# One DMA queue for loads and stores, with longer store runs and shorter load runs, in a FiLM scale-and-shift kernel

## The chip, the cores and the metric

The kernel runs on one core of a Trainium2 chip. The metric is the device time of one execution in microseconds (us), as the median of several executions. The profile's span is shorter than that time by some 1.8 us in the profiled run of the kernel before (84.35 against 82.6). Some executions of this one-core kernel fall in a slower state (from 85.8 us up, over 1.5% above the fastest of the same kernel); they are set aside, and only fast runs are compared.

## The reference

```python
def reference(x, conditioning, gamma_proj, beta_proj):   # x: 32 x 512 x 256, float32
    gamma = conditioning @ gamma_proj                    # 32 x 64 times 64 x 256
    beta = conditioning @ beta_proj
    return (x * (1 + gamma[:, None, :]) + beta[:, None, :]).astype(np.float32)
```

Each of 32 batches has one row of scales and one of shifts. The arithmetic is one multiplication and one addition for each element; the bulk of the work is to bring 16.78 MB in and 16.78 MB out.

## The kernel before

The input is cut into four slabs of 4 MB. In a slab each of 128 partitions holds 32 rows of 256 floats, contiguous in memory, so a slab is 32 KB for each partition. All four slabs have their own place on the chip, so no load waits for a buffer.

```python
LOADS = {0: [8, 24]}                 # rows of each load; a slab not listed: one load of 32 rows
GROUP = 16; ON_DVE = 11
...
for n in LOADS.get(s, [ROWS]):       # all loads on the SyncE queue
    nc.sync.dma_start(out=xs[:, r : r + n, :], in_=x_v[s, :, r : r + n, :])
...                                  # scales and shifts: a short chain of matmuls
for r0 in range(0, ROWS, GROUP):     # two groups of 16 rows in each slab
    v = xs[:, r0 : r0 + ON_DVE, :]               # 11 rows on VectorE
    w = xs[:, r0 + ON_DVE : r0 + GROUP, :]       # 5 rows on GpSimd
    nc.vector.scalar_tensor_tensor(out=v, in0=rows(g_p, nv), scalar=1.0, in1=v,
                                   op0=ALU.add, op1=ALU.mult)
    nc.gpsimd.tensor_tensor(out=w, in0=w, in1=rows(g_s, nw), op=ALU.mult)
    nc.vector.tensor_add(out=v, in0=v, in1=rows(b_p, nv))
    nc.gpsimd.tensor_tensor(out=w, in0=w, in1=rows(b_s, nw), op=ALU.add)
    nc.scalar.dma_start(out=o_v[s, :, r0 : r0 + GROUP, :],       # stores on the ScalarE queue
                        in_=xs[:, r0 : r0 + GROUP, :])
```

A row is 1 KB, so a load of 8, 24 or 32 rows moves runs of 8, 24 or 32 KB for each partition, and a store of 16 rows moves runs of 16 KB. In the packet records such a run is one packet, and each of the 16 DMA engines carries 8 of a transfer's 128.

## Time and profile before

| | before |
|---|---|
| time, median of 3 | 84.59 us (84.4 to 85.89; the last in the slower state) |
| span of the profiled run | 82.6 us |
| packet time of the two queues, share of 16 engines | 48.6% + 48.0% |
| VectorE and GpSimd busy | 60% and 56% |
| last VectorE instruction ends | 66.6 us |
| last store packet ends | 81.4 us |

The table is read from the bottom up. Compute is over 15 us before the last byte is out, and the DMA engines are full throughout. The lines themselves are in the prediction. A second source beside the page is used there: the trace has a start and a duration for each of the 2080 DMA packets. I call a load packet *stretched* by what it took over the undisturbed time of its size, and give the sum of this over all packets divided by 16, which is the stretch for each engine.

### The profile page before, as it was taken

Reading aid. Unit: us, or ns where it says so; the run is one execution under the profiler, and the core shown is the slowest. Engines: PE = TensorE matmul, PEld = TensorE weight load, DVE = VectorE, ACT = ScalarE, POOL = GpSimd, SP = SyncE. Lnnn points to the kernel's source line nnn. Section 1 sums busy time; section 2 is a strip of 40 time slices with the busy share of each in tenths; the row PEclk is TensorE's granted clock in tenths of the full one; section 3 lists DMA queues with packets and bytes.
Section 4 is the critical chain, followed back from the end, with each engine's and each line's share of the span. In section 5 each row is a group of like instructions: output and inputs, shape, how many; then the busy total and the mean of one; then the engine's idle time right before and its main releaser. Section 6 shows DMA issues by size and latency. Waiting matters only on the chain.

```text
span 82.6 us, 156 instructions
## 1 busy us (share of the span) xinstructions
PE 9.1 (11%) x10; PEld 2.8 (3%) x10; DVE 49.9 (60%) x18; ACT 3.9 (5%) x9; POOL 46.2 (56%) x22
## 2 busy tenths in 40 slices
PE   0080000899600000000000000000000000000000
PEld 0100000443000000000000000000000000000000
DVE  2011000059999999999999999999999920000000
ACT  0600000034400000000000000000000000000000
POOL 2000000069999999999999999999995000000000
DMA  3899999969969989998889979899999999999992
GB/s 56 337 508 397 389 397 524 460 302 508 508 270 492 508 381 381 413 476 381 381 381 556 460 302 460 381 468 421 429 452 389 468 421 421 460 389 452 437 421 87
DMA packets 2080, 33.69 MB, mean 408 GB/s; under 512 B 288, under 2 KB 416, under 8 KB 416
## 3 DMA queue, kind: packets, MB, share of 16 engines
q1 hardware_dynamic: 720, 16.78, 48.6%
q10 hardware_dynamic: 1360, 16.92, 48.0%
HBM read 16.92 MB, written 16.78 MB: 408 GB/s over the span
## 4 chain that ended last, share of the span: by engine, by line
DVE 49%; DMA 16%; issue 11%; PE 2%; ACTq 1%; ACT 1%
DVE xs L100 30%; DVE xs L103 19%; DMA gbproj<-in_beta_proj_dram 16%; PE gb_p L79 2%; ACTq L50 1%; ACTq L48 0%; ACT gb_s L82 0%; ACT gb_s L85 0%
## 5 line engine op out<-in xcount | busy, mean ns | idle before, releaser
L102 POOL TENSOR_TENSOR xs<-xs,gb_s 128x1280 f32<-128x1280 f32 x8 | 23.0, 2895 | 16.2 <-ACT gb_s L82 16.2
L100 DVE SCALAR_TENSOR_TENSOR xs<-gb_p,xs 128x2816 f32<-128x2816 f32 x8 | 24.7, 3083 | 10.9 <-ACT gb_s L85 10.9
L103 DVE TENSOR_TENSOR xs<-xs,gb_p 128x2816 f32<-128x2816 f32 x8 | 24.7, 3086 | 0.3
L104 POOL TENSOR_TENSOR xs<-xs,gb_s 128x1280 f32<-128x1280 f32 x8 | 23.0, 2893 | 0.0
L79 PE MATMUL gb_p<-gbproj,cond_T 64*128 64x512 f32 x8 | 7.2, 1074 | 8.9 <-DMA gbproj<-in_beta_proj_dram 8.9
L74 DVE COPY cond_T<-cond_T_p 64x512 f32<-64x512 f32 x1 | 0.7, 683 | 4.3 <-PE cond_T_p L72 4.3
L79 PEld LDWEIGHTS gb_p<-gbproj,cond_T 64*128 64x128 f32 x8 | 2.5, 328 | 13.7 <-issue 13.7
L72 PE MATMUL cond_T_p<-rident,cond_s 32*64 32x512 f32 x2 | 1.9, 1065 | 3.9 <-DMA cond_s<-in_conditioning_dram 3.9
L82 ACT ACTIVATE gb_s<-gb_p 128x256 f32<-128x256 f32 x4 | 1.5, 383 | 16.4 <-PE gb_p L79 16.4
L85 ACT COPY gb_s<-gb_p 128x256 f32<-128x256 f32 x4 | 1.5, 367 | 0.0
L82 ACT ACT_TABLE_LOAD x1 | 1.3, 1283 | 2.4 <-issue 2.4
L67 DVE COPY rident<-ident 32x512 f32<-32x512 f32 x1 | 0.4, 416 | 1.2 <-POOL ident masks.py:199 1.2
L72 PEld LDWEIGHTS cond_T_p<-rident,cond_s 32*64 32x64 f32 x2 | 0.3, 202 | 3.9 <-issue 3.9
masks.py:197 POOL MEMSET ident<- 32x32 f32 x1 | 0.1, 114 | 0.3 <-POOLq L121 0.3
masks.py:199 POOL TENSOR_SCALAR_AFFINE_SELECT ident<-ident 32x32 f32<-32x32 f32 x1 | 0.2, 202 | 0.1
L121 POOL MEMSET const-float32-0.0<- 128x1 f32 x1 | 0.1, 103 | 0.2 <-issue 0.2
L121 POOL MEMSET const-bfloat16-1.0<- 128x1 bf16 x1 | 0.1, 106 | 0.0
L121 POOL MEMSET const-uint8-127<- 128x1 uint8 x1 | 0.1, 106 | 0.0
L121 POOL MEMSET const-float32-1.0<- 128x1 f32 x1 | 0.1, 103 | 0.0
## 6 DMA issues: line engine op xcount, KB each, us to landing
out_dram<-xs ACTq DMA_DIRECT2D x8, 2048.0 KB, 18.2
xs<-in_x_dram SPq DMA_DIRECT2D x3, 4096.0 KB, 32.9
xs<-in_x_dram SPq DMA_DIRECT2D x1, 3072.0 KB, 12.2
xs<-in_x_dram SPq DMA_DIRECT2D x1, 1024.0 KB, 4.6
gbproj<-in_gamma_proj_dram ACTq DMA_DIRECT2D x1, 64.0 KB, 9.1
gbproj<-in_beta_proj_dram ACTq DMA_DIRECT2D x1, 64.0 KB, 12.9
cond_s<-in_conditioning_dram ACTq DMA_DIRECT2D x1, 8.0 KB, 3.0
```

The source lines that it names most:

```text
L50: nc.scalar.dma_start(out=gbproj[:, :dim], in_=gamma_proj)
L67: nc.vector.tensor_copy(out=rident.rearrange("p (b g) -> p b g", g=REP), in_=ident.to_broadcast([batch, batch, REP]),)
L72: nc.tensor.matmul(cond_T_p, lhsT=cond_s, rhs=rident, start=True, stop=True)
L74: nc.vector.tensor_copy(out=cond_T, in_=cond_T_p)
L79: nc.tensor.matmul(p_t, lhsT=cond_T[:, s * P : (s + 1) * P], rhs=gbproj, start=True, stop=True)
L82: nc.scalar.activation(out=s_t[:, :dim], in_=p_t[:, :dim], func=mybir.ActivationFunctionType.Identity, bias=1.0, scale=1.0)
L85: nc.scalar.copy(out=s_t[:, dim:], in_=p_t[:, dim:])
L100: nc.vector.scalar_tensor_tensor(out=v, in0=rows(g_p, nv), scalar=1.0, in1=v, op0=ALU.add, op1=ALU.mult)
L102: nc.gpsimd.tensor_tensor(out=w, in0=w, in1=rows(g_s, nw), op=ALU.mult)
L103: nc.vector.tensor_add(out=v, in0=v, in1=rows(b_p, nv))
L104: nc.gpsimd.tensor_tensor(out=w, in0=w, in1=rows(b_s, nw), op=ALU.add)
L121: nc = _bacc.Bacc("TRN2", target_bir_lowering=False, num_devices=1)
```

## The change

The intent is to let loads and stores no longer compete: with all transfers on one queue, the loads come first and the stores follow. The two middle slabs are loaded in two pieces each, so that compute can start on the first half sooner, and stored whole, in fewer and longer runs.

```diff
-    LOADS = {0: [8, 24]}
+    LOADS = {0: [8, 24], 1: [16, 16], 2: [16, 16]}
+    STORES = {0: (16, 32), 3: (16, 32)}
@@
-            nc.scalar.dma_start(out=o_v[s, :, r0 : r0 + GROUP, :],
-                                in_=xs[:, r0 : r0 + GROUP, :])
+            if (r0 + GROUP) in STORES.get(s, (ROWS,)):
+                e0 = max([0] + [e for e in STORES.get(s, (ROWS,)) if e <= r0])
+                e1 = r0 + GROUP
+                nc.sync.dma_start(out=o_v[s, :, e0:e1, :], in_=xs[:, e0:e1, :])
```

## The prediction

> **What bounds the kernel now.** I read the utilisation part of the page first, then the table of DMA queues, then the stretches of the span, then the DMA view cut to three windows, and only then the chain of work that ended last, because the chain alone misleads here.
>
> ```profile
> span 82.6 us, 156 instructions
> ...
> DVE  2011000059999999999999999999999920000000
> ...
> POOL 2000000069999999999999999999995000000000
> DMA  3899999969969989998889979899999999999992
> ...
> q1 hardware_dynamic: 720, 16.78, 48.6%
> q10 hardware_dynamic: 1360, 16.92, 48.0%
> HBM read 16.92 MB, written 16.78 MB: 408 GB/s over the span
> ```
>
> The two compute engines stop two thirds of the way through and start late; the DMA row is full from the second slice to the last but one. The two queues (q1 carries the loads of SyncE, q10 the constants and the stores of ScalarE) together took 48.6 + 48.0 = 96.6% of sixteen engines' span: 0.966 x 82.6 = 79.8 us of packet time on each DMA engine. What is left, 2.8 us, is at the two ends:
>
> ```profile
> 0.00:2.00 2.00, 0.00 (x0) 0.00 (x0) 0.42 (x1) 0.00 (x0) 0.53 (x6) 1.00 0.29 53
> ...
> 48.00:80.00 32.00, 0.00 (x0) 0.00 (x0) 18.48 (x7) 0.00 (x0) 14.97 (x6) 1.00 1.01 431
> 80.00:81.40 1.40, 0.00 (x0) 0.00 (x0) 0.00 (x0) 0.00 (x0) 0.00 (x0) 1.00 0.63 269
> 81.40:82.60 1.20, 0.00 (x0) 0.00 (x0) 0.00 (x0) 0.00 (x0) 0.00 (x0) 1.00 0.00 0
> ```
>
> The columns are the stretch, its length, the busy time of five engines, the clock, and at the end the DMA share and GB/s. The first packet starts near 1.3 us, the last store packet ends at 81.4 us, and 1.2 us pass before the span ends. So between 1.3 and 81.4, which is 80.1 us, an engine's packets fill 79.8: about 0.3 us of true gaps. The clock outside the span is 84.35 (the profiled run) less 82.6, or 1.75 us.
>
> The chain names VectorE for half the span, but it ends with the last VectorE instruction at 66.6 us (63.49 start plus 3.09); the last store was issued at 66.7 and landed 15.1 us later, since it stood in a queue. The kernel is bound by DMA bytes, with compute ahead of the queue.
>
> **What the Trainium skill says, and whether the trace agrees.** "DMA: Bandwidth & Descriptors", section Specifications, gives a fabric ceiling of 435 GB/s for the sixteen engines; the trace's fully used stretch shows 431, so it agrees. The same page, section Issuing engines are not separate DMA queues, says that transfers from several issuing engines run on the same 16 DMA engines and interleave, and that only issue time is saved. That agrees too: in the window 24 to 48 us the loads hold 72.7% and the stores 25.5%, with no more than 100% between them. Its section Queues, rings and completion order says that an engine goes round robin between queues by packet and takes one queue's descriptors in order; so with everything on one queue I expect all loads first, then stores. The trace before fits the first half (loads and stores share that window), but cannot show the second. "Perfetto Trace Analysis", section DMA Optimizations, suggests giving inputs and outputs different issuing engines when the spread is dynamic, which is what before does and the change undoes; no run here shows yet what that is worth.
>
> **The three regimes in the trace before.** The windows 2 to 24, 24 to 48 and 48 to 80 us are loads alone, loads and stores mixed, and stores alone:
>
> ```profile
> DMA packets 659, 9.47 MB, mean 430 GB/s; under 512 B 128, under 2 KB 256, under 8 KB 256
> ```
> ```profile
> DMA packets 416, 9.96 MB, mean 415 GB/s; under 512 B 32, under 2 KB 32, under 8 KB 32
> ...
> q1 hardware_dynamic: 240, 7.34, 72.7%
> q10 hardware_dynamic: 176, 2.62, 25.5%
> ```
> ```profile
> DMA packets 953, 13.78 MB, mean 431 GB/s; under 512 B 112, under 2 KB 112, under 8 KB 112
> ```
>
> The reader is to see 430, 415 and 431 GB/s. Packets are counted whole where they start, so an edge misplaces up to half a megabyte; the 415 is softer than it looks. The trace's record of single packets is sharper. An undisturbed load packet takes 309 ns for 8 KB, 912 for 24 KB and 1213 for 32 KB; the 1024 store packets of 16 KB take 611. All four lie on one line, 7.7 ns + 37.67 ns per KB (16 KB: 7.7 + 602.7 = 610.4). Load packets of 32 KB longer than 1213 ns cost 0.57 us in sum for each engine: about 0.12 at 12 to 14 us, beside the constants, and 0.45 at 24 to 34 us, around the arrival of the first store (issued 25.9, first packet 29.8).
>
> **The change part by part.**
>
> *Splitting two slabs' loads into 16 KB runs.* Each DMA has 8 packets on each engine. Two 32 KB loads become four of 16 KB: 16 packets become 32 on each engine. By the line above that adds 16 x 7.7 ns = 0.12 us.
>
> *Whole-slab stores for the middle slabs.* Four 16 KB stores become two of 32 KB: 32 packets become 16, which removes 16 x 7.7 ns = 0.12 us. The completion packets (9 ns each) go from 8 to 6 for the stores and from 5 to 7 for the loads. The sum of these parts is zero; the total stays 2080 packets.
>
> *One queue.* The loads no longer share with stores. Their packets: 8 x 0.365 (the 8 KB ones as measured, start-up included) + 8 x 0.937 + 32 x 0.611 + 8 x 1.213 = 2.92 + 7.50 + 19.55 + 9.70 = 39.7 us, plus 0.5 for the constants and 1.3 for the start: all loads are in by about 41.5 us, where before the last ended at 48.6. Then come 32 x 0.611 + 16 x 1.213 = 39.0 us of stores, to 80.5, plus the 0.3 of gaps and 0.1 of completion packets: 80.9, against 81.4. If all the disturbance at 24 to 34 us goes, the gain is 0.45 us; it began before the first store packet ran, so I count on half or a little more, 0.3 to 0.4.
>
> *Readiness.* The order of instructions in the changed build interleaves slabs on VectorE (multiply of the next group ahead of the add of the last). VectorE begins an instruction each 3.065 us from 17.52 (the last of 16 begins at 63.49), so the n-th ends at 17.52 + 3.065(n-1) + 3.09. GpSimd ends its share earlier: it starts at 17.3, 2.85 apart, and its last ends at 63.0. The stores' last operands are GpSimd's third and VectorE's fifth, ninth, 12th, 14th and 16th instruction: ready at 25.9, 32.9, 45.1, 54.3, 60.5 and 66.6. The queue reaches them at 41.5, 46.4, 51.3, 61.0, 70.7 and 75.6 (4.9 us for 2 MB, 9.7 for 4 MB). The slack is 15.6, 13.5, 6.2, 6.7, 10.2 and 9.0 us. The first constant took 3.0 us from issue to landing with little ahead of it, so a start of 2 to 3 us fits inside the smallest. The whole-slab store costs slack, not time. The changed build's waits show no store waiting for another store.
>
> *Start.* The second projection lands at 14.6 us because its packets alternate with 24 and 32 KB load packets; with 16 KB runs it may land up to 1 us sooner. Compute is not on the bounding path, so this only adds slack.
>
> The sum: 84.59 - 0.4 = **84.2 us**.
>
> **The rivals.**
>
> 1. *The queue runs dry.* A store waits in order on SyncE, so the second slab's store, kept back until the whole slab is done, could leave the engines idle and delay all after it. For it: a 4 MB store needs both groups, and VectorE's reordering puts the first group's add behind the next slab's multiply. Against: 6.2 us of slack, and no wait of compute for x data in the trace. If compute started 5 us late and start-up took 2, about 1 us would be lost: 85 to 86.
>
> 2. *Mixing was a cost, and separating it pays more.* For: 415 against 430 GB/s. Taken at face value, 9.96 MB would take 23.1 instead of 24.0 us, and 0.9 us would be won: 83.7. Against: the packet records allow only 0.45 us there. Even with every disturbance gone, 0.57 + 0.20 (24 KB packets) + 0.45 (8 KB packets), the gain is 1.2 us: 83.4, still within 2%.
>
> 3. *Mixing was a help, or one queue is worse than two.* Two queues could hide a gap of one behind the other. Against: with stores alone q10 holds 100.5% of the engines, and with loads almost alone q1 100.6%. The switch from loads to stores on the same ring is new; I allow it 0.5 us: 84.8.
>
> 4. *SyncE is blocked issuing,* because a queue holds only so many descriptors. It would issue later, but only while the queue is full: no change.
>
> **Range and chances.** The gain cannot pass 1.2 us by the packet sums, so faster by over 2% (under 82.9) needs something the trace does not show: 3%. Slower by over 2% (over 86.3) needs rival 1 with two of its slacks wrong, or a new cost of one ring: 5%. Within 2%: 92%. Runs of before scatter from 84.4 to 85.89, so the range is wider upward: 83.5 to 85.3.
>
> **What would show each step right or wrong.** Right: q1 carries 33.5 MB in about 1872 packets and q10 0.14 MB in 208; the sum of packet time is 79.2 to 79.8 us on an engine; the DMA row stays full to the last slice but one; loads are done near 41.5 us and no store packet runs before; packets of 16 KB take 611 ns as loads too; the last store is issued near 66.7 us and lands 14 to 15 us later. Wrong: a slice of low DMA share between 41 and 76 us (rival 1, if a store is issued right then; rival 3, if the stores had long been issued); load packets still above 1213 ns at 24 to 34 us (the disturbance was not the mixing); a last packet before 80 us (rival 2 or more). A longer end after the last packet, or compute beginning much after 17.5 us, would also break the sum.

## The result, and the profile after

The changed kernel takes 84.52 us (median of six, 84.37 to 87.42) against 84.53 us for the kernel before (median of six). The ratio is 1.0 with a 95% interval of 0.9981 to 1.002. Ratios here are not quite the ratio of the quoted medians. The change is worth less than 0.2% either way.

The utilisation part and the queue table of the changed kernel's page:

```profile
span 82.6 us, 155 instructions
...
DVE  2002000079999999999999999999999700000000
...
DMA  2899999999999999988969999988999998899991
...
q1 hardware_dynamic: 1872, 33.56, 95.9%
q10 hardware_dynamic: 208, 0.14, 0.5%
```

The plan was carried out. Queue q1, that of SyncE, now carries everything but the constants, in the 1872 packets that were foreseen. The two shares add to 96.4%, where they were 96.6%: 0.2% of 82.6 us, less than 0.2 us of packet time, is all that was saved. VectorE ends about 1 us earlier, which the time does not show.

The stretches of the span that answer to those shown of before, and the three regimes, now loads alone (2 to 24 us, and on to 42), and stores alone (from 42 us on); the last two columns are the DMA share and GB/s:

```profile
0.00:2.00 2.00, 0.00 (x0) 0.00 (x0) 0.41 (x1) 0.00 (x0) 0.53 (x6) 1.00 0.28 45
2.00:24.00 22.00, 9.10 (x10) 2.78 (x10) 7.66 (x4) 3.87 (x9) 7.23 (x3) 1.00 1.00 419
24.00:42.00 18.00, 0.00 (x0) 0.00 (x0) 18.00 (x7) 0.00 (x0) 17.84 (x7) 1.00 1.00 422
42.00:48.00 6.00, 0.00 (x0) 0.00 (x0) 6.00 (x3) 0.00 (x0) 5.92 (x3) 1.00 0.99 423
48.00:80.00 32.00, 0.00 (x0) 0.00 (x0) 17.45 (x6) 0.00 (x0) 14.85 (x6) 1.00 1.01 433
80.00:81.40 1.40, 0.00 (x0) 0.00 (x0) 0.00 (x0) 0.00 (x0) 0.00 (x0) 1.00 0.66 281
81.40:82.60 1.20, 0.00 (x0) 0.00 (x0) 0.00 (x0) 0.00 (x0) 0.00 (x0) 1.00 0.00 0
```

There is no idle stretch between 2 and 80 us, the same start and the same tail of 1.2 us. The packet records, here and below those of one profiled execution of each kernel, say where the hoped-for gain went:

| each engine, us | before | after |
|---|---|---|
| stretch at 0 to 5 us (first packets) | 0.45 | 0.49 |
| stretch at 5 to 16 us (beside the constants) | 0.32 | 0.26 |
| stretch at 26 to 46 us | 0.45 | 0.38 |
| stretch later | 0 | 0 |
| sum of packet time | 79.76 | 79.67 |
| last packet ends at | 81.39 | 81.42 |

In the kernel before, the stretched load packets at 26 to 46 us are those that start at 28.4 to 28.7 us, just ahead of the first store packet (0.26 us up to 32 us), and again those that start at 32.2 to 32.7 us, when two store packets have gone by on each engine (0.19 us). From 36 to 46 us loads and stores share the engines and every load packet takes the undisturbed 1213 ns. In the changed kernel the stretched packets are the last load packet on each engine, the one ahead of the first store packet. Three engines from the packet records of the changed kernel, from 39.5 us on (start in us, L for the loads' and stores' queue, size in KB or * for a completion packet, the one of 4 bytes that closes a transfer on an engine, ns). The records do not name the engine; a packet is put behind the one whose end it meets within 4 ns:

```
39.53L32:1213 40.74L32:1481 42.21L*:9 42.22L16:611 42.83L16:611
39.64L32:1213 40.85L32:1302 42.15L*:9 42.15L16:611 42.76L16:611
39.63L32:1213 40.84L32:1762 42.60L*:9 42.61L16:611 43.21L16:611
```

The packets of 32 KB before 42 us are loads, those of 16 KB stores. So the cost was not removed; it moved from 28 us to 41 us, to the place where stores now begin.

### The profile page after: what moved, and what is told of

It reads as the page before. It is cut to its first block, busy times and chain, and to the rows that moved or that the text cites. A ratio compares the mean times of both kernels' runs of the same rounds, so it can differ in the third digit from the quotient of the medians.

```text
span 82.6 us, 155 instructions
## 1 busy us (share of the span) xinstructions
PE 9.1 (11%) x10; PEld 2.8 (3%) x10; DVE 49.5 (60%) x18; ACT 3.9 (5%) x9; POOL 46.4 (56%) x22
## 3 DMA queue, kind: packets, MB, share of 16 engines
q1 hardware_dynamic: 1872, 33.56, 95.9%
## 4 chain that ended last, share of the span: by engine, by line
DVE 48%; DMA 15%; issue 11%; PE 2%; ACTq 1%; ACT 1%
DVE xs L101 29%; DVE xs L104 19%; DMA gbproj<-in_beta_proj_dram 15%; PE gb_p L80 2%; ACTq L51 1%; ACTq L49 0%; ACT gb_s L83 0%; ACT gb_s L86 0%
```

## The experiments

The first question is why one queue gained nothing. **Theory A**: what is stretched is the load packets in flight when the first store begins, once in an execution, whichever queue the store is on (A2); a variant has each passage from load to store cost that much (A1), or only where the packets are long (A3). **Theory B**: queue and sizes have effects of opposite sign that cancel. The second question is whether the slack that the prediction worked out for the whole-slab stores is real. Medians include slow runs; ratios do not.

### The queue alone

```diff
 (kernel before)
-            nc.scalar.dma_start(out=o_v[s, :, r0 : r0 + GROUP, :],
+            nc.sync.dma_start(out=o_v[s, :, r0 : r0 + GROUP, :],
```

> The kernel before with one part of the change alone: its eight 16 KB-run stores issued by SyncE behind the loads, sizes untouched. Theory A (one switch costs what the mixing cost: the last load packet on each engine before the first store packet is stretched, whichever queue the store is on): 84.5 us, within 0.3% of before, with some 0.4 us of stretched load packets for each engine, all of it at 40 to 43 us, and packet time of 79.7 us for each engine. Theory B (queue and sizes have opposite effects that cancel in the full change): the queue alone would show 84.1 us or less.

Measured: 84.65 us against 84.55, ratio 1.0004 (0.9981 to 1.0027). The packet time is 79.85 us for each engine, and the stretch at 40 to 43 us is 0.54 us, with none between 16 and 40. Theory B falls for this part: the queue alone does nothing to the time.

### The sizes alone

```diff
 (changed kernel)
-                nc.sync.dma_start(out=o_v[s, :, e0:e1, :], in_=xs[:, e0:e1, :])
+                nc.scalar.dma_start(out=o_v[s, :, e0:e1, :], in_=xs[:, e0:e1, :])
```

> The other part alone: the new load and store sizes, stores left on the ScalarE queue. Theory A: 84.5 us, within 0.3% of before, the stretched load packets come in the first microseconds after the first store packet (28 to 36 us) and add up to 0.3 to 0.5 us for each engine. Theory B (opposite effects): 84.9 us or more here.

Measured: 84.53 us against 84.55, ratio 0.9989 (0.9968 to 1.001). The profiled run was slow, so it was run again for one look:

> The run with the new sizes and the old store queue again, since its profile fell in the slow state: 84.5 us, with 0.3 to 0.5 us of stretched load packets for each engine in the first microseconds after the first store packet and none later, as theory A said.

Measured: 84.28 us, a single run. The stretch after 26 us is 0.13 us, nearly all of it at 28 to 32 us, where the stores begin: the right place, but under the 0.3 to 0.5 that I expected. The gain is not the 0.3 us that this might suggest, as 0.52 us of stretch stands at 5 to 16 us in this run, where before had 0.32. Theory B asked for 0.4 us off with the queue alone and 0.4 us on with the sizes alone; both are outside the intervals, so it is out.

### One passage and five passages from load to store

Both kernels cut the last slab's load and the first slab's stores into four pieces of 8 KB runs. In the control, all loads come first; in the other, each of those stores is followed by one of those loads.

```diff
 (changed kernel; the last slab's load is taken out of the loop of loads)
-                nc.sync.dma_start(out=o_v[s, :, e0:e1, :], in_=xs[:, e0:e1, :])
+                if s == 0:
+                    for q in range(e0, e1, 8):
+                        nc.sync.dma_start(out=o_v[0, :, q : q + 8, :], in_=xs[:, q : q + 8, :])
+                        nc.sync.dma_start(out=slabs[3][:, q : q + 8, :], in_=x_v[3, :, q : q + 8, :])
+                else:
+                    nc.sync.dma_start(out=o_v[s, :, e0:e1, :], in_=xs[:, e0:e1, :])
```

The control has the last slab's loads in the loop of loads, with `3: [8] * 4` in LOADS, and not in this place.

> Control for the next run: the changed kernel with the last slab loaded in four pieces of 8 KB runs and the first slab stored in four such pieces, loads still all ahead of stores. By the packet line of the prediction (7.7 ns for each packet) 40 more packets on each engine cost 0.31 us and four more completion packets 0.04: 84.85 us. Stretched load packets: about 0.4 us for each engine, once, near 42 us. All theories of the stretch say the same here.

Measured: 84.83 us, ratio 1.0024 (1.0003 to 1.0046); packet time 79.91 us, stretch at 40 to 44 us 0.16 us. The added packets cost 0.2 to 0.3 us, where the line of the prediction says 0.35; with an interval of 0.2 us either way, this run does not tell that line from the smaller cost found below.

> The same pieces as the control, but on the queue each of the first slab's four stores is followed by one of the last slab's four loads, so an engine passes from load to store five times and back four times instead of passing once. Theory A1 (each passage from load to store costs about 0.4 us): 5 x 0.38 = 1.9 us of stretch, 1.5 us over the control, 86.3 us. Theory A2 (only the first stores cost it, later passages are free): 84.8 us as the control, stretch 0.4 us in all. The prediction's first idea (mixing in itself costs) would give an amount in between that grows with the time mixed, 84.9 to 85.3 us.

Measured: 84.89 us, ratio 1.0037 (1.002 to 1.0053), 0.1 us over the control by the means (84.87 and 84.77). The stretch is 0.30 us at 28 to 32 us, ahead of the first store, and 0.03 us at 32 to 40, where the next passages are. Theory A1 asked for 1.9 us of stretch and 86.3 us; it is out. The time alone does not settle the idea that mixing costs, which began at 84.9 us; the packet records do, since loads were stretched by only 0.03 us while they alternated with stores.

### Two passages with long packets

The later passages of the five had 8 KB packets, which the changed kernel has not. So the last slab's load, with its 32 KB runs, was put behind the first slab's two stores.

```diff
 (changed kernel; the last slab's load is taken out of the loop of loads)
                 nc.sync.dma_start(out=o_v[s, :, e0:e1, :], in_=xs[:, e0:e1, :])
+                if s == 0 and e1 == ROWS:
+                    nc.sync.dma_start(out=slabs[3], in_=x_v[3])
```

> The changed kernel with one edit: the last slab's 4 MB load is issued after the first slab's two stores, so an engine passes from load to store twice, the second time from a 32 KB load packet, as in the changed kernel. Theory A2 (the stretch of load packets comes once, at the first store): stretch near 0.3 to 0.4 us for each engine at about 31 us (from 16 KB packets) and under 0.05 us at the second passage near 51 us; 84.5 us. Rival A3 (the later passages of the five-switch run were free only because their packets were 8 KB): another 0.3 us or more at the second passage and 84.9 us.

Measured: 84.53 us against 84.51, ratio 0.9993 (0.9973 to 1.0014). The stretch is 0.17 us at 28 to 36 us, ahead of the first store, and 0.001 us after 46 us, where the second passage is. The same passage, from 32 KB load packets to a store, stretched loads by 0.38 us in the changed kernel, where it was the first. So A3 is out. A2 stands for later passages on one queue, but its "once" is too strong for the kernel before, where the second group of stretched packets comes two store packets after the first; the slowed kernel before, below, has the same two groups (0.21 and 0.18 us). What the runs show is a cost around the first few store packets, gone some 4 us after the first of them, and not one that grows with the time mixed. Its size was below the 0.3 to 0.4 that I expected here, and it varies between runs.

### Slower compute, in both kernels: the slack

VectorE takes 13 of 16 rows in place of 11, so that compute ends some 8 us later, while the DMA work is unchanged.

```diff
-    ON_DVE = 11
+    ON_DVE = 13
```

> The changed kernel with 13 of 16 rows on VectorE in place of 11, a test of the slack. A VectorE instruction goes from 3.06 to 3.62 us apart; from 17.0 the fifth, ninth, 12th, 14th and 16th end at 35.1, 49.6, 60.4, 67.7 and 74.9 us. The queue reaches these stores at 46.7, 51.6, 61.3, 71.0 and 75.9. If the slack is as worked out and a store needs 2 us from issue to its first packet, the 12th and the 16th come 1 us late each at most: 84.5 to 86.5 us, with a dip in the DMA row near 61 to 63 or 75 to 77 us. If the stores were in truth already near the bound, the whole 8.3 us by which compute ends later would show: up to 92 us.

Measured: 86.77 us, ratio 1.0288 (1.0246 to 1.0331), just above the range that I gave. Stretches of its span:

```profile
60.00:62.00 2.00, 0.00 (x0) 0.00 (x0) 2.00 (x1) 0.00 (x0) 0.00 (x0) 1.00 0.61 262
62.00:64.10 2.10, 0.00 (x0) 0.00 (x0) 2.10 (x2) 0.00 (x0) 0.00 (x0) 1.00 0.00 0
64.10:66.00 1.90, 0.00 (x0) 0.00 (x0) 1.90 (x1) 0.00 (x0) 0.00 (x0) 1.00 1.29 552
...
74.00:76.00 2.00, 0.00 (x0) 0.00 (x0) 0.00 (x0) 0.00 (x0) 0.00 (x0) 1.00 0.92 393
76.00:78.00 2.00, 0.00 (x0) 0.00 (x0) 0.00 (x0) 0.00 (x0) 0.00 (x0) 1.00 0.92 393
```

And the timeline of the same run around the issue of the third slab's store:

```profile
59.60 7.14 DVE L104 TENSOR_TENSOR xs<-xs,gb_p 128x3328 f32<-128x3328 f32 x2
63.29 0.33 SPq L109 DMA_DIRECT2D out_dram<-xs  x1
```

All 16 engines are idle from 62.0 to 64.1 us. VectorE has two additions in a row from 59.60; the first, which is the 13th of its 16 large instructions, ends at 63.2 us and completes the third slab; SyncE issues the store at 63.29, and its first packet starts at 64.13. That is one gap of 2.1 us, and the span is 84.9 us, 2.3 us over 82.6. My expectation was off because I had taken the order of VectorE's instructions from the changed kernel, where the third slab is completed by the 12th. With the new split, the build put the last slab's first multiplication ahead of it, and the slab was complete at 63.2 us, 2.8 us later than the 60.4 that I had worked out. A last store that comes late did not happen, since the gap ahead of it had already pushed the queue back.

The same slowing in the kernel before:

> The kernel before with 13 of 16 rows on VectorE, to be held against the changed kernel with the same slowing (86.77 us, engines idle from about 61 to 64 us while the third slab's whole store waited for its second group). Theory C (the coarse store in one ordered queue uses up slack that the kernel before has): here the third slab goes out in two stores, the first ready ten instructions in (about 53 us) and the second 13 in (63.5 us), by when the queue still holds work to about 65 us; only the last store (ready near 74 us, queue empty near 74.7) comes late, by a microsecond or less: 84.6 to 85.6 us. Rival (slow compute costs both kernels the same): 86.5 us or more.

Measured: 84.55 us, ratio 1.0013 (0.9997 to 1.003).

```profile
60.00:62.00 2.00, 0.00 (x0) 0.00 (x0) 2.00 (x2) 0.00 (x0) 0.00 (x0) 1.00 1.07 459
62.00:64.00 2.00, 0.00 (x0) 0.00 (x0) 2.00 (x1) 0.00 (x0) 0.00 (x0) 1.00 0.97 418
```

VectorE finishes the third slab in the same place, 13th, near 64 us, and the engines do not stop. With compute 8 us longer the kernel before takes the time that it took without. So the change did cost something that the time does not show: slack. The last run asks which part.

```diff
 (slowed changed kernel)
-    STORES = {0: (16, 32), 3: (16, 32)}
+    STORES = {s: (16, 32) for s in range(4)}
```

> The slowed changed kernel with one part of the change undone: the middle slabs go out in two 16 KB-run stores each, as before, still all on the SyncE queue behind the loads. If the whole-slab store is what used up the slack (theory C1), the third slab's first half is ready near 53 us and keeps the engines busy past 63.2 us, when the second is ready: no idle stretch, 84.5 to 85.0 us as in the slowed kernel before. If the single ordered queue is the cause (theory C2), it stays near 86.8 us with the engines idle near 62 to 64 us.

Measured: 84.97 us, ratio 1.0052 (1.0029 to 1.0075). With half-slab stores on the single queue, 1.8 of the 2.2 us that the slowing had cost are back; the whole-slab store is the cause, and the queue is not more than a small part. The profiled run was slow (86.0 us of span), so how the remaining 0.4 us over the slowed kernel before arises was not read from a trace and stays open. The slow profile shows no idle stretch between 60 and 78 us; that is a weak sign, since its slower loads had pushed the queue back by then.

### The cost of short runs

```diff
-    LOADS = {0: [8, 24], 1: [16, 16], 2: [16, 16]}
+    LOADS = {s: [4] * 8 for s in range(4)}
```

> The changed kernel with all loads cut into 32 DMAs of 4 KB runs. Theory of the prediction (a packet costs 7.7 ns plus 37.67 ns per KB): an engine's load packets rise from 56 to 256, so 200 x 7.7 = 1.54 us more, and 25 more completion packets of 9 ns, 0.22 us: 84.5 + 1.8 = 86.3 us, and a 4 KB packet lasts 158 ns. Rival (run length does not matter above some KB, the line is an accident of four points): 84.5 us. Rival (SyncE is held by the waits of 32 issues and starves the engines): a DMA row with gaps, and more than 86.5 us.

Measured: 85.61 us, ratio 1.0126 (1.0099 to 1.0153). The 4 KB packets took 180 ns on average:

> The run with 4 KB loads again, since its profile fell in the slow state: time 85.5 us; the packet records should show 4 KB packets at some 160 ns and not the mean of 180 ns of the slow profile. If the sum of packet time is about 81 us, packets set the time; if it is under 80 us, gaps between packets do.

Measured: 85.66 us, a single run, with this on its page:

```profile
span 83.9 us, 189 instructions
...
DMA  2899999999999999999999999999999999899990
...
q1 hardware_dynamic: 5472, 33.56, 96.6%
```

A 4 KB packet takes 159 ns, and the line of the prediction gives 158. The sum of packet time is 81.5 us for each engine, 1.8 us over the changed kernel, as worked out. But the last packet ends only 1.13 us later (82.55 against 81.42), and the time rose by only 1.1 us: 81.5 us of packets stand in 80.8 us between the first and the last (1.75 to 82.55), so the records of neighbouring packets overlap: on an engine a packet's record starts 3 to 4 ns before that of the one ahead ends. A packet's added cost, as the end of the run shows it, is nearer 5 ns (an estimate: 1.13 us less 0.22 for completion packets, over 200) than 7.7. SyncE did not starve the engines; the DMA row has no gap. The stretch ahead of the first store is under 0.001 us here: with 4 KB loads it was absent from this one profile.

### An attempt at a faster version

```diff
-    LOADS = {0: [8, 24], 1: [16, 16], 2: [16, 16]}
+    LOADS = {}
```

> The changed kernel with every slab loaded by one DMA of 32 KB runs, the first slab too. In the trace of the changed kernel an engine spends 8 x 0.370 + 8 x 0.931 = 10.4 us on the first slab in runs of 8 and 24 KB; in runs of 32 KB it would be 8 x 1.213 = 9.7 us if the start-up stretch vanishes and 10.2 if it stays; 32 fewer 16 KB load packets become 16 of 32 KB, another 0.12 us less. If packet time sets the end: 83.8 to 84.3 us. If compute starting later (the first slab's and the second projection's arrival near 16 us in place of 14.2) sets it: 84.5 us or more; the slack of 6 us says it does not.

Measured: 84.64 us, ratio 1.0005 (0.9985 to 1.0025): no gain. The packet time fell from 79.67 to 79.49 us, less than expected, because the stretch of the first packets grew from 0.49 to 0.63 us, and the last packet ends at 81.47 us, no sooner. No faster arrangement of the same bytes was found; the queue alone, the sizes alone, both, and this one stand within 0.2% of each other.

## Why the prediction was right, and where its working was not

**What bounds the kernel** was right. Slowing compute by 8 us left the kernel before at 84.55 us, and adding 1.8 us of packet time to the changed kernel made it slower by 1.1 us.

**The sizes** were right: their sum of zero is confirmed by the sizes-only run at a ratio of 0.9989, and 16 KB load packets take 611 ns, the same as 16 KB stores. The cost of a packet as it reaches the end is smaller than the line says, some 5 in place of 7.7 ns.

**The queue** is the step that failed. It said: "If all the disturbance at 24 to 34 us goes, the gain is 0.45 us; it began before the first store packet ran, so I count on half or a little more, 0.3 to 0.4." The gain is 0.01 us in the medians, with an interval of about 0.2 us either way. The disturbance was taken for a cost of mixing loads with stores. It comes around the first store packets, and the changed kernel has those too, so 0.45 us at 28 to 34 us became 0.38 us at 41 to 42 us. A closer look at the trace before could have told it: the kernel before mixes loads and stores from 36 to 46 us too, and there no load packet is stretched. The window of the step was too wide as well: the first stretched packets start at 28.4 us and end as the first store packets start, from 29.8 us on. The sign set for this step would have misled: it looked for long load packets at 24 to 34 us, where the changed kernel has none, and not at the place to which they moved. The sum beside the step, 80.9 against 81.4 us, agreed with the gain by accident: it starts at 1.3 us where the first packet starts at 1.74 us in the kernel before and 1.76 in the changed one, and it adds 0.3 us of gaps where the records overlap. So the loads were done at 42.1 to 42.6 us, not 41.5. That the range held the result is no merit of this step: the forecast was only 0.4 us on 84.6, and a gain of nothing lay inside the range.

**Rival 2** (mixing was a cost, more would be won) fell with the same finding, as its 415 GB/s for the mixed window was for the most part the edge effect of whole packets (the packets counted in it fill a share of 0.98, those of the 430 GB/s window 1.03) and the start of the stores. **Rival 3** (one queue is worse than two) fell as well: its 0.5 us for the passage from load to store does appear as 0.38 us of stretch, but the kernel before pays the same.

**Readiness and rival 1** were right. The stores were issued at 25.4, 32.3, 44.3, 53.4, 60.1 and 65.6 us, each up to 1 us ahead of the working, as the second projection landed 0.5 us sooner and VectorE's instructions followed each other 3.03 us apart in place of 3.065, and no engine ran dry. The allowance of 2 to 3 us from issue to first packet was too large: in the slowed run, with the queue empty, it was 0.84 us (63.29 to 64.13). The step "The whole-slab store costs slack, not time" is the one that the experiments bear out most sharply: slack of some 7.5 and 8 us was there in the changed kernel (the whole-slab stores were issued at 44.3 and 53.4 us and their first packets start from 51.8 and 61.5 us on), and once VectorE's 13 of 16 rows and a changed order of instructions had used it up, the loss was 2.2 us, where the kernel before lost nothing.

**Rival 4** (SyncE blocked) left no mark on the time: SyncE issued its last load at 5.5 us and then waited for compute.

## What to carry to other kernels

Where the DMA engines were full from end to end, moving transfers between queues or reordering them did not change the time (within 0.2% here); first add up the packet time for each engine and see whether the change removes any. A disturbance seen where two streams meet may belong to the beginning of one of them: look whether it goes on as long as they share the engines, before crediting its removal to a change that separates them. A larger store saves little (by an estimate under 0.1 us for the two here: 16 packets fewer on each engine, at some 5 ns) and holds back its first half until the second is ready, so check the slack behind it against the order of instructions in the build, and check again when the split of work changes.

## What the Trainium skill lacked or had wrong

- "DMA: Bandwidth & Descriptors", section Queues, rings and completion order, holds: on one queue every engine finished its loads before its first store packet, near 42 us. No page tells of the stretch of the last load packets when stores begin: 0.13 to 0.54 us for each engine from run to run with packets of 16 and 32 KB ahead of it, 0.16 us with 8 KB, none with 4 KB, and at later passages on one queue 0.03 us or less. In the kernel before, with two queues, 0.19 of its 0.45 us came after two store packets. What causes it was not found.
- "Perfetto Trace Analysis", section DMA Optimizations, suggests, above all where there are loops or control flow, one issuing engine for inputs and another for outputs. In this kernel, with full DMA engines, it is worth nothing: 84.65 us with all on one, 84.55 us with two, ratio 1.0004.
- The same section says that larger DMAs help and names steps from 2 KB to 4 or 8 KB. It gives no figure for longer runs: loads of 4 KB runs cost 85.61 us against 84.52 for runs of 8 to 32 KB; undisturbed packets take 159, 309, 611, 912 and 1213 ns for 4, 8, 16, 24 and 32 KB.
- Executions of the changed kernel were 84.37 to 84.7 us, and one 87.42 us, with the granted TensorE clock at 1.0 (full speed) in both. The slow profiles show where the time goes: in the one with 4 KB loads a load packet takes 178 ns in the median against 159, in the one of the slowed kernel with half-slab stores 681 against 611 for 16 KB and 1351 and more against 1213 for 32 KB, while store packets keep their 611 ns.
